# First projection of a decoder trunk: stationary operand from a transposed read of x, the norm's scale put on v, q and k afterwards

## The chip, the cores and the metric

One core of one Trainium2 chip runs the whole program in one launch. The metric is the device time of one execution in microseconds. TensorE is called PE here, its weight loads PEld, VectorE DVE, ScalarE ACT, GpSimd POOL, and the queue that issues most DMAs is SyncE's (SP).

## The reference

The model has two layers over 512 tokens of width 1024. Only the head of layer 0 matters here: an RMSNorm with gain `g[0]`, one projection to q, k, v and 16 forget-gate logits, and attention with 16 heads of width 64.

```
def rmsnorm(x, g):
    y = xf * lax.rsqrt(jnp.mean(xf * xf, axis=-1, keepdims=True) + RMS_EPS)
    return (y * g)

hn = rmsnorm(x, g[0])
proj = hn @ w_in                     # q | k | v | forget logits
q = q * HEAD_DIM ** -0.5
log_f = log_sigmoid(proj[..., 3 * D:] + b_f);  c = cumsum(log_f)
s = q k^T + c_q - c_k, causal;  o = softmax(s) @ v;  return o @ w_out
```

After it come the output projection, an MLP, a gated embedding, and the second layer with a short convolution in the place of attention. All of that is untouched by the change.

## The kernel before, in words

Everything is float32, and every product is taken as three products of halves: a value is split into a rounded high part (`hi`, made by ACT) and a rest (`lo`, made by DVE as source minus `hi`), and `mm3` (L212) issues hi·hi, lo·hi and hi·lo into one accumulator. A weight tile goes the same way: SP fetches a `raw` tile (`fetch`, L113, 14 buffers), and `prepare` (L133) splits it into `wh` and `wl`. `wide` (L150) prepares a tile and up to `soon` tiles ahead of it. SBUF pages of 128x512 come from one pool of 70, PSUM accumulators from 8 banks.

The projection needs the activations with the model width on the partitions. So before the change, for each of the four blocks of 128 tokens, ACT sums the squares of a row-major x tile (`squares`, L243), POOL makes the reciprocal root (`rstd`, L234), DVE multiplies x by it and by the gain (`scaled`, L251), PE turns eight 128x128 squares (`turned`, L259), and ACT and DVE split the result into `hT` (`keep`, L265), a pair of tiles of 128 x 8 x 512. The gain `g0` is spread over the partitions by two PE matmuls of a row of ones with a row of g (L856 to L858), for which POOL's queue loads two rows.

v is made in three column chunks (`V_CHUNKS`, L32): columns 768 to 1023 with the 16 logits (272 wide), 0 to 511 (512 wide), 512 to 767 (256 wide). In each, the token block is stationary and the weight moves: 8 k-tiles x 4 token blocks x 3 products, 96 matmuls. The first chunk is ordered by hand (`manual_schedule`, L568) for PE, DVE and ACT: block t runs its first five k-tiles, then block t+1 is turned, then block t ends. All that follows is ordered by a scheduler that simulates the engines and may move an instruction that is ready ahead of earlier ones in the program.

`keep_v` (L400) adds the bias to the logits and splits v out of PSUM in pieces of 128 columns. `logs` and `sums_of_logs` make the cumulated gates; `bias` loads them, spread over the partitions, for each head. `project(i)` (L418) makes k and then q of a head pair, 24 matmuls of 512 columns each, ACT and DVE splitting each out of PSUM; pairs 1 to 7 are streamed in between the scores, transposes and mixes of the heads.

DMAs at the start are ordered by hand (L850): the first x block by ACT's and SP's queues, then weight tiles and the other x blocks on SP.

Of the kernel before, what the change touches and what calls it, by code (L numbers as in the profile page):

```python
# [8 lines left out]
F32 = mybir.dt.float32  # L9
F32R = mybir.dt.float32r  # L10
AF = mybir.ActivationFunctionType
ALU = mybir.AluOpType
# [3 lines left out]
P = 128  # L16
D = 1024
S = 512
H = 16
HD = 64  # L20
# [18 lines left out]
SCORED = 12  # L39
LEFT = 10  # L40
LATE = 0

# [16 lines left out]


@with_exitstack
def trunk(ctx: ExitStack, tc, x, pT, g, wv, wqk, bf, wo, wci, cw, wco, wup, wdn, wpp, wpg, out):
    nc = tc.nc
    pool = lambda name, bufs, **k: ctx.enter_context(tc.tile_pool(name=name, bufs=bufs, **k))
    consts = pool("consts", 1)
# [10 lines left out]
    def bank(name):  # L78
        return psum.tile([P, S], F32, tag="ps", name=name)
# [70 lines left out]
    def wide(*key, soon=SOON):  # L150

        prepare(where[key] + 1 + soon)
        return ready[key]
# [58 lines left out]
    def mm3(ps, a, b, start, stop):  # L212

        nc.tensor.matmul(ps, a.hi, b.hi, start=start, stop=False)  # L214
        nc.tensor.matmul(ps, a.lo, b.hi, start=False, stop=False)  # L215
        nc.tensor.matmul(ps, a.hi, b.lo, start=False, stop=stop)  # L216
        streamed[0] += 3 * ps.shape[-1]
        due()

    def split(hi, lo, src, eng=nc.vector):  # L220

        nc.scalar.copy(hi, src)  # L222
        eng.tensor_tensor(out=lo, in0=src, in1=hi.bitcast(F32), op=ALU.subtract)  # L223

    def gain(l, i):
        ts = [page(f"g{l}_{i}_{n}") for n in range(2)]
        for n in range(2):
            nc.sync.dma_start(
                ts[n][:, :S],
                g[6 * l + i : 6 * l + i + 1, n * S : (n + 1) * S].partition_broadcast(P),  # L230
            )
        return ts
# [15 lines left out]
    def stats(t, xs, name):  # L248
        return rstd([squares(xs[n][:, :S], f"{name}_q{n}_{t}") for n in range(2)], f"{name}_r{t}")

    def scaled(t, n, xs, r, gB, name):  # L251
        h = page(f"{name}_h{t}_{n}")
        nc.vector.scalar_tensor_tensor(
            out=h[:, :S], in0=xs[n][:, :S], scalar=r, in1=gB[n][:, :S],
            op0=ALU.mult, op1=ALU.mult,
        )
        return h

    def turned(t, n, h, name):  # L259
        ps = bank(f"{name}_p{t}_{n}")  # L260
        for j in range(4):
            nc.tensor.transpose(ps[:, j * P : (j + 1) * P], h[:, j * P : (j + 1) * P], ident)
        return ps

    def keep(t, n, ps, hT):  # L265
        to = lambda h: h[:, 4 * n : 4 * n + 4, t * P : (t + 1) * P]
        split(to(hT.hi), to(hT.lo), ps.rearrange("p (j c) -> p j c", j=4))
# [33 lines left out]
    def load_x(name, t):  # L301
        xs = [page(f"{name}{t}_{n}") for n in range(2)]
        for n in range(2):
            eng = nc.scalar if name == "xa" and n else nc.sync
            eng.dma_start(xs[n][:, :S], x[t * P : (t + 1) * P, n * S : (n + 1) * S])
        return xs

    def tokens_of(pair, t):
# [2 lines left out]
    def tokens(pair, k, t):  # L311
        return pair.at(lambda h: h[:, k, t * P : (t + 1) * P])
# [20 lines left out]
                         f"{kind}r")  # L333
                then(t)

    def attention(hT, first_x, g0, by_hand):
        b_f = consts.tile([P, H], F32, tag="bf", name="b_f")

        vs = [[page(f"v{t}_{i}", F32R) for i in range(4)] for t in range(NB)]
# [43 lines left out]
                )  # L383
                nc.sync.dma_start(neg_c[b, :, :n], t[:H, :n])

        def values(c, t, soon=SOON, between=None):

            c0, width = V_CHUNKS[c]
            n_v = min(width, D - c0)
            ps = bank(f"v{c}_{t}")  # L390
            for k in range(KT):
                if width == 256:
                    w = wide("v", c, k // 2).at(lambda u: u[:, k % 2 * 256 : k % 2 * 256 + 256])
                else:
                    w = wide("v", c, k, soon=soon)
                if k == 5 and between:
                    between()
                mm3(ps[:, :width], tokens(hT, k, t), w, k == 0, k == KT - 1)

            def keep_v():  # L400
                if n_v < width:
                    nc.vector.tensor_tensor(
                        out=logit[:, t * H : (t + 1) * H], in0=ps[:, n_v:width], in1=b_f,
                        op=ALU.add,
                    )
                for c1 in range(0, n_v, 256):
                    src = ps[:, c1 : c1 + 256].rearrange("p (i e d) -> p i e d", e=2, d=HD)
                    block = vs[t][(c0 + c1) // 256].rearrange("p (i r) -> p i r", i=2)
                    for e in range(2):
                        hi = block[:, :, 192 * e : 192 * e + HD]  # L410
                        lo = block[:, :, 64 + 64 * e : 128 + 64 * e]
                        split(hi, lo, src[:, :, e, :])

            return keep_v

        stacked, probs, outs, both = {}, {}, {}, {}

        def project(i):  # L418

            q, key = (Pair(page(f"{n}h{i}", F32R), page(f"{n}l{i}", F32R)) for n in "qk")  # L420
            stacked[i] = q, key
            for s in (1, 0):
                ps = bank(f"qk{i}_{s}")
                for k in range(KT):
                    mm3(
                        ps, narrow("qk", i, k=k, c=s * P),
                        hT.at(lambda h: h[:, k, :]), k == 0, k == KT - 1,
                    )
                    if k < KT - 1:
                        yield  # L430
                if s == 0:
                    nc.scalar.mul(q.hi[:, :S], ps, HD**-0.5)
                    nc.vector.scalar_tensor_tensor(
                        out=q.lo[:, :S], in0=ps, scalar=HD**-0.5, in1=q.hi[:, :S].bitcast(F32),
                        op0=ALU.mult, op1=ALU.subtract,
                    )
                else:
                    split(key.hi[:, :S], key.lo[:, :S], ps)
                yield
# [114 lines left out]
            yield from out_part((0, 1), (6,))  # L554

        nc.sync.dma_start(b_f, bf[0:1, :].partition_broadcast(P))
        name = "n0"
        E, done_v = mybir.EngineType, []

        def rows(t):  # L560
            r = stats(t, first_x[t], name)
            return [scaled(t, n, first_x[t], r, g0, name) for n in range(2)]

        def turn_rows(t, hs):
            for n in range(2):
                keep(t, n, turned(t, n, hs[n], name), hT)

        with tc.manual_schedule(engines={E.PE, E.DVE, E.Activation}):  # L568
            r = stats(0, first_x[0], name)
            prepare(3)  # L570
            hs = {0: [scaled(0, n, first_x[0], r, g0, name) for n in range(2)]}
            prepare(4)
            for n in range(2):
                keep(0, n, turned(0, n, hs[0][n], name), hT)
                prepare(5 + n)
            prepare(KT)
            hs[1] = rows(1)
            hs[2] = rows(2)
            for t in range(NB):
                between = (lambda: turn_rows(t + 1, hs[t + 1])) if t + 1 < NB else None  # L580
                done_v.append(values(0, t, 0, between))
                if t + 3 < NB:
                    hs[t + 3] = rows(t + 3)
                if t:
                    prepare(KT + 3 * t)
                    done_v.pop(0)()
        done_v.pop(0)()
        tri = page("tri", F32R)
        ones = page("ones")
        nc.gpsimd.memset(ones[:, :S], 1.0)  # L590
# [4 lines left out]
        nc.vector.tensor_copy(tri[:, :S], ones[:, :S])  # L595
        logs()
        for t in range(NB):
            values(1, t)()
            if t == 2:
                sums_of_logs(tri)  # L600
        bias(0)
        bias(1)
        for t in range(NB):
            values(2, t)()
        for _ in project(0):
            pass
        main = stream()
# [234 lines left out]
                then(t)  # L842


    one = page("one")
    nc.vector.memset(one[:1, :P], 1.0)
    rows = [page(f"row{n}") for n in range(2)]
    for n in range(2):
        nc.gpsimd.dma_start(rows[n][:1, :], g[0:1, n * S : (n + 1) * S])
    with tc.manual_schedule(engines={mybir.EngineType.SP, mybir.EngineType.Activation}):  # L850
        first_x = [load_x("xa", 0)]
        fetch(4)
        first_x.append(load_x("xc", 1))
        fetch(KT)
        first_x += [load_x("xc", t) for t in (2, 3)]
    g0 = [bank(f"g0_{n}") for n in range(2)]  # L856
    for n in range(2):
        nc.tensor.matmul(g0[n], one[:1, :P], rows[n][:1, :], start=True, stop=True)  # L858
    kept = dram.tile([2, NB, 2, P, S], F32, tag="kept", name="kept")
    hT = turned_x  # L860
    by_hand = ExitStack()
    lhs, opened = attention(hT, first_x, g0, by_hand)
    oT = lhs
    lhs = lambda k, t: tokens(oT, k, t)
    kind = "o"
# [45 lines left out]
def layout(x, p, norm_g, w_attn_in, b_forget, w_attn_out, w_conv_in, conv_w, w_conv_out,  # L911
# [17 lines left out]
    ).reshape(D, 2 * D)  # L929
    got["wqk"] = tiles(qk, 2, 256)  # L930
    got["bf"] = np.asarray(b_forget)
    got["wo"] = tiles(np.asarray(w_attn_out)[0], 1, S)
    b, c, u = (np.asarray(w_conv_in)[0].reshape(D, 3, KT // 2, 2, P)[:, s] for s in range(3))
    ci = np.stack([c[:, :, 0], u[:, :, 0], b[:, :, 0], b[:, :, 1], c[:, :, 1], u[:, :, 1]], axis=2)
# [27 lines left out]
```

## Time and profile before

| what | value |
|---|---|
| median of three runs | 1263.35 us (1263.23 to 1263.46) |
| span of the profiled execution | 1262.1 us |
| what lies around the span (median less span) | 1.25 us |
| PE busy | 1238.7 us, 98% of the span |
| DVE, ACT, POOL busy | 906.1, 604.0, 627.5 us |
| mean granted TensorE clock | 0.997 |
| HBM read, written | 136.93 MB, 6.37 MB |

The profile is one execution. Its span runs from the first instruction to the last. A timeline row gives the start, the length, the engine, the line and the tiles; `x8` means that eight instructions are merged. A matmul's length holds its way through the array and overlaps the next one's, so what one costs in a row of many is the distance between starts.

### The profile page before, as it was taken

The page shows a single profiled execution, that of the slowest core. Times are in us where ns is not written, and L with a number is a line of the kernel's source. Part 1 is how long each engine was busy: PE and PEld are TensorE (multiplying, and loading weights), DVE is VectorE, ACT ScalarE, POOL GpSimd, SP SyncE. Part 2 cuts the span into 40 slices and gives each one's busy share as a digit, 9 for nine tenths or more (in the row PEclk, how much of TensorE's full clock was granted, in tenths as well). Part 3 has the DMA queues.
Part 4 walks back from the last instruction along what each step waited for, and adds up shares of the span by engine and source line. Part 5 has one row for each costly group of instructions (what it writes and reads, how often), then busy time and mean ns, then how long its engine had stood idle before and what let it go on. Part 6 is the DMA issues. An engine that isn't in the chain of part 4 may idle for free.

```text
span 1262.1 us, 18000 instructions
## 1 busy us (share of the span) xinstructions
PE 1238.7 (98%) x6036; PEld 1022.3 (81%) x6036; DVE 906.1 (72%) x1386; ACT 604.0 (48%) x1293; POOL 627.5 (50%) x631
## 2 busy tenths in 40 slices
PE   7999999999999999999999999999999999999997
PEld 6877777788888888888789988889788888888876
DVE  5645666767788788879867444457778897779973
ACT  5445656654645434554455333344653445535451
POOL 2027555328787777876211000016777777878210
PEclk9999999999999999999999999999999999999999
DMA  7554342161432244227333233432323442235401
GB/s 249 152 142 149 100 126 76 62 224 65 134 95 86 87 134 134 84 68 258 126 100 94 74 101 101 141 124 86 94 74 101 134 130 84 71 117 175 159 18 50
DMA packets 83228, 144.48 MB, mean 114 GB/s; under 512 B 9600, under 2 KB 16816, under 8 KB 83136
## 3 DMA queue, kind: packets, MB, share of 16 engines
q1 hardware_dynamic: 82928, 143.07, 36.3%
q8 instruction: 47, 0.77, 0.2%
q14 instruction: 45, 0.37, 0.1%
q10 hardware_dynamic: 144, 0.26, 0.1%
q0 software_dynamic: 64, 0.00, 0.0%
HBM read 136.93 MB, written 6.37 MB: 114 GB/s over the span
## 4 chain that ended last, share of the span: by engine, by line
PE 60%; DVE 18%; POOL 7%; issue 6%; ACT 6%; DMA 3%; SPq 1%; DVEq 0%; POOLq 0%; ACTq 0%
DVE wl L223 10%; POOL s L720 4%; PE up L215 3%; PE up L216 3%; PE up L214 3%; ACT wh L222 3%; PE dn L215 3%; PE qk L214 3%; PE dn L216 3%; PE dn L214 3%; DVE acc L752 2%; PE qk L216 2%; PE qk L215 2%; PE sc L468 2%; PE pg L214 2%
## 5 line engine op out<-in xcount | busy, mean ns | idle before, releaser
L223 DVE TENSOR_TENSOR wl<-raw,wh 128x512 fp32r<-128x512 f32 (+1 forms) x404 | 365.2, 955 | 25.3 <-ACT wh L222 24.6
L222 ACT CAST wh<-raw 128x512 fp32r<-128x512 f32 (+1 forms) x404 | 219.5, 619 | 8.9 <-DVE xd L296 5.0
L215 PE MATMUL up<-hTh,wl 128*128 128x512 f32 (+1 forms) x576 | 210.5, 366 | 0.0
L216 PE MATMUL up<-hTl,wh 128*128 128x512 f32 (+1 forms) x576 | 210.0, 366 | 0.0
L214 PE MATMUL up<-hTh,wh 128*128 128x512 f32 (+1 forms) x576 | 209.7, 366 | 0.0
L223 POOL TENSOR_TENSOR wl<-T,wh 128x512 fp32r<-128x512 f32 x112 | 160.9, 1468 | 35.8 <-ACT wh L222 32.0
L215 PEld LDWEIGHTS up<-hTh,wl 128*128 128x128 f32 x576 | 108.7, 189 | 17.6
L214 PEld LDWEIGHTS up<-hTh,wh 128*128 128x128 f32 x576 | 108.6, 189 | 17.5
L216 PEld LDWEIGHTS up<-hTl,wh 128*128 128x128 f32 x576 | 108.3, 189 | 17.3
L752 DVE TENSOR_TENSOR acc<-dn,acc 128x512 f32<-128x512 f32 x168 | 107.4, 679 | 10.5 <-PE dn L216 10.5
L131 POOL TENSOR_TENSOR T<-raw,raw 128x512 f32<-128x512 f32 x56 | 87.5, 1573 | 37.0 <-DMA raw<-in_wdn 24.8
L706 ACT ACTIVATE r<-up 128x512 f32<-128x512 f32 (+1 forms) x72 | 38.7, 547 | 126.3 <-PE up L216 126.3
L131 POOL TENSOR_TENSOR T<-raw,T 128x512 f32<-128x512 f32 x56 | 91.3, 1631 | 2.2
L692 DVE TENSOR_TENSOR q<-r 128x512 f32<-128x512 f32 (+1 forms) x72 | 66.9, 936 | 29.2 <-ACT r L706 29.2
L237 POOL TENSOR_SCALAR cor_r_v<-cos,cos 128x1 f32<-128x1 f32 x4 | 1.6, 398 | 159.1 <-ACT junk L245 159.1
L222 ACT CAST wh<-T 128x512 fp32r<-128x512 f32 x112 | 61.2, 617 | 0.0
L222 ACT CAST A11h<-q 128x256 fp32r<-128x256 f32 x28 | 11.4, 407 | 99.9 <-DVE q L692 99.9
L214 PE MATMUL pg<-wh,hTh 128*128 128x512 f32 x128 | 50.9, 398 | 3.4 <-ACT hTh L222 3.3
L214 PE MATMUL qk<-hTh,wh 128*128 128x512 f32 x128 | 53.0, 414 | 0.0
L759 POOL TENSOR_TENSOR acc<-acc,acc 128x512 f32<-128x512 f32 x28 | 47.0, 1708 | 10.0 <-DVE acc L752 10.0
L216 PE MATMUL qk<-hTl,wh 128*128 128x512 f32 x128 | 50.8, 397 | 0.0
L215 PE MATMUL qk<-hTh,wl 128*128 128x512 f32 x128 | 50.5, 395 | 0.0
(236 smaller groups left out, 3067.1 us busy)
## 6 DMA issues: line engine op xcount, KB each, us to landing
raw<-in_wup SPq DMA_DIRECT2D x128, 256.0 KB, 2.9
raw<-in_wdn SPq DMA_DIRECT2D x128, 256.0 KB, 2.8
raw<-in_wci SPq DMA_DIRECT2D x48, 256.0 KB, 3.5
raw<-in_wqk SPq DMA_DIRECT2D x32, 256.0 KB, 3.8
raw<-in_wpg SPq DMA_DIRECT2D x32, 256.0 KB, 3.8
g<-in_g SPq DMA_DIRECT2D x22, 256.0 KB, 5.4
prl<-neg_c SPq DMA_DIRECT2D x16, 256.0 KB, 6.7
raw<-in_wo SPq DMA_DIRECT2D x16, 256.0 KB, 2.7
```

The lines of the kernel that those rows point to most:

```text
L131: nc.gpsimd.tensor_tensor(out=B[name, p], in0=B[a, p], in1=B[b, p], op=ALU.subtract)
L214: nc.tensor.matmul(ps, a.hi, b.hi, start=start, stop=False)
L215: nc.tensor.matmul(ps, a.lo, b.hi, start=False, stop=False)
L216: nc.tensor.matmul(ps, a.hi, b.lo, start=False, stop=stop)
L222: nc.scalar.copy(hi, src)
L223: eng.tensor_tensor(out=lo, in0=src, in1=hi.bitcast(F32), op=ALU.subtract)
L468: nc.tensor.matmul(ps[:, :nm], at[r, b * P : n], to[r, :nm], start=s == 0, stop=s == 2)
L692: nc.vector.tensor_tensor(out=out, in0=r, in1=r, op=ALU.mult)
L706: nc.scalar.activation(r[:, :n], ps[:, :n], AF.Relu)
L720: sums = lambda out, a, b, op: nc.gpsimd.tensor_tensor(out=out, in0=a, in1=b, op=op)
L752: nc.vector.tensor_tensor(out=a, in0=banks[s], in1=a, op=ALU.add)
L759: nc.gpsimd.tensor_tensor(out=a, in0=a, in1=acc[i, s][:, :S], op=ALU.add)
```

## The change

The host also hands in x transposed (`xT`, eight tiles of 128 x 512, one for each k-tile, 256 KB each) and the first gain as a column table `g0T`. `hT` for k-tile k is now `xT[k]` times the gain of each partition: ACT multiplies and rounds to `hi`, DVE makes `lo` from the same source (`split_by`). The scale per token is left out of it. The first two v chunks keep four accumulators open, one for each token block, and go k-tile by k-tile (`chunk`): 12 matmuls for each. Row-major x is still loaded, behind the first eight weight tiles, and its sums of squares and `r0[t]` are made during the second chunk. `keep_v` multiplies by `r0[t]`. The four `r0` columns are also written to a DRAM row and read back spread over the partitions as `r_row`, and `project` multiplies q's and k's accumulator by it on DVE into an SBUF page, from which ACT and DVE then split. The row of ones, the gain rows and their matmuls, the 32 transposes of the first norm and their splits are gone. PE gets 16 matmuls of a zeroed page at the very start. The sums of logs move from behind the third block of chunk 2 to behind the second block of chunk 3, and chunk 3 is made block by block behind all of the second chunk's `keep_v`.

```diff
+WARM = 16
+    def split_by(hi, lo, src, by):
+        nc.scalar.mul(hi, src, by)
+        nc.vector.scalar_tensor_tensor(
+            out=lo, in0=src, scalar=by, in1=hi.bitcast(F32), op0=ALU.mult, op1=ALU.subtract
+        )
...
+        def keep_v(c, t, ps):
...
+                nc.vector.scalar_tensor_tensor(
+                    out=logit[:, t * H : (t + 1) * H], in0=ps[:, n_v:width], scalar=r0[t],
+                    in1=b_f, op0=ALU.mult, op1=ALU.add,
+                )
...
+                    split_by(hi, lo, src[:, :, e, :], r0[t])
...
+                scaled_ps = page(f"qk{i}_{s}")[:, :S]
+                nc.vector.tensor_tensor(out=scaled_ps, in0=ps, in1=r_row[:, :S], op=ALU.mult)
+                ps = scaled_ps
...
+        def chunk(c, after):
+            width = V_CHUNKS[c][1]
+            banks = [bank(f"v{c}_{t}") for t in range(NB)]
+            for k in range(KT):
+                if c == 0:
+                    split_by(hT.hi[:, k, :], hT.lo[:, k, :], first_xT[k][:, :S], g0_col[:, k : k + 1])
+                w = wide("v", c, k, soon=0)
+                for t in range(NB):
+                    mm3(banks[t][:, :width], tokens(hT, k, t), w, k == 0, k == KT - 1)
+                after(k)
+            return banks
...
         with tc.manual_schedule(engines={E.PE, E.DVE, E.Activation}):
-            r = stats(0, first_x[0], name)
...
+            banks = {0: chunk(0, lambda k: None)}
+            def between(k):
+                t = k - 1
+                if 0 <= t < NB:
+                    r0[t] = stats(t, first_x[t], "n0")
+                    nc.sync.dma_start(
+                        r_dram[0:1, t * P : (t + 1) * P].rearrange("o s -> s o"), r0[t]
+                    )
+                    if t == NB - 1:
+                        nc.sync.dma_start(r_row[:, :S], r_dram[0:1, :].partition_broadcast(P))
+                if k >= NB:
+                    keep_v(0, k - NB, banks[0][k - NB])
+            banks[1] = chunk(1, between)
...
         for t in range(NB):
-            values(1, t)()
-            if t == 2:
+            keep_v(1, t, banks[1][t])
+        for t in range(NB):
+            values(2, t)
+            if t == 1:
                 sums_of_logs(tri)
         bias(0)
         bias(1)
-        for t in range(NB):
-            values(2, t)()
...
+    warm = page("warm")
+    nc.vector.memset(warm[:, :S], 0.0)
...
+        nc.scalar.dma_start(g0_col, g0T)
+        for k in range(KT):
+            (nc.scalar if k < 2 else nc.sync).dma_start(first_xT[k][:, :S], xT[k])
+            fetch(k + 1)
+        first_x = []
+        for t in range(NB):
+            fetch(KT + t + 1)
+            first_x.append(load_x("xc", t))
+    idle = bank("idle")
+    for _ in range(WARM):
+        nc.tensor.matmul(idle[:, :P], warm[:, :P], warm[:, :P], start=True, stop=True)
```

## Rows read from the trace of the kernel before

**Rows 1.** Waits of PE: engine, line, what for, total us, times, longest.

```profile
PE g L858 <- DMA row<-in_g: 6.0, 1, 6.0
```

**Rows 2.** Windows: length, busy us of each engine, granted clock, DMA share, GB/s.

```profile
11.43:65.59 54.16, 52.14 (x322) 47.19 (x321) 35.08 (x87) 28.95 (x77) 6.58 (x16) 0.97 0.60 193
65.59:300.00 234.41, 232.59 (x1244) 182.16 (x1243) 153.60 (x384) 132.94 (x331) 113.51 (x177) 1.00 0.39 123
300.00:1240.00 940.00, 934.26 (x4403) 778.91 (x4402) 707.35 (x899) 434.13 (x868) 502.72 (x424) 1.00 0.35 108
1240.00:1262.10 22.10, 14.23 (x63) 11.46 (x61) 6.98 (x10) 3.37 (x8) 1.72 (x4) 0.93 0.12 47
```

**Rows 3.** Timeline of PE over the projection of v: start us, length us, then names.

```profile
5.96 3.75 PE L858 MATMUL g<-row,one 1*128 1x512 f32 x4 [5.96 <-DMA row<-in_g]
...
11.43 0.59 PE L214 MATMUL v<-wh,hTh 128*128 128x272 f32 x1
...
13.00 0.35 PE L215 MATMUL v<-wh,hTl 128*128 128x272 f32 x1
...
16.50 1.96 PE L262 MATMUL n_p<-ident,n_h 128*128 128x128 f32 x8 [1.89 <-DVE n_h L253]
...
18.72 0.43 PE L216 MATMUL v<-wl,hTh 128*128 128x272 f32 x1
...
19.62 0.43 PE L214 MATMUL v<-wh,hTh 128*128 128x272 f32 x1
...
33.06 0.30 PE L216 MATMUL v<-wl,hTh 128*128 128x272 f32 x1
...
35.70 0.29 PE L216 MATMUL v<-wl,hTh 128*128 128x272 f32 x1
...
47.38 0.40 PE L371 MATMUL ps_c<-tri,lf_h 128*16 128x512 f32 x1
...
48.55 0.44 PE L214 MATMUL v<-wh,hTh 128*128 128x512 f32 x1
48.84 0.39 PE L215 MATMUL v<-wh,hTl 128*128 128x512 f32 x1
...
54.08 0.28 PE L214 MATMUL v<-wh,hTh 128*128 128x256 f32 x1
...
65.59 0.40 PE L214 MATMUL qk<-hTh,wh 128*128 128x512 f32 x1
```

**Rows 4.** DMA from 0 to 30 us: rate in 40 slices of 0.75 us; one issue.

```profile
GB/s 0 0 19 48 143 380 383 383 400 370 371 317 328 351 238 249 287 361 355 402 404 407 404 393 391 377 348 379 382 268 74 0 0 22 22 224 153 265 341 52
...
xa<-in_x SPq DMA_DIRECT2D x1, 256.0 KB, 4.4
```

**Rows 5.** ACT and DVE prices near the new operations: min/median/max ns, or busy us, mean ns.

```profile
L664 ACT ACTIVATE za<-z,taps x10: 508/724/725, 690.6 to 807.4; 128x512 f32<-128x512 f32 x6, 128x256 f32<-128x256 f32 x4
...
L253 DVE SCALAR_TENSOR_TENSOR n_h<-xc,n_r_y,g 128x512 f32<-128x512 f32 x6 | 4.2, 745 | 3.4 <-POOL n_r_y L240 3.3
...
L223 DVE TENSOR_TENSOR wl<-raw,wh 128x272 fp32r<-128x272 f32 x8 | 3.2, 436 | 6.4 <-ACT wh L222 6.4
```

**Rows 6.** Timelines of SP and ACT: a DMA of line 637, weight casts, a piece of v.

```profile
16.09 0.33 SPq L637 DMA_DIRECT2D taps<-in_cw  x1
...
38.73 2.69 ACT L222 CAST wh<-raw 128x512 fp32r<-128x512 f32 x5
...
46.52 0.27 ACT L222 CAST v<-v 128x128 fp32r<-128x128 f32 x1 [0.36 <-DVE v L223]
```

**Rows 7.** Timelines of DVE and PE: q of pair 1 ready, its first score.

```profile
91.52 0.69 DVE L433 SCALAR_TENSOR_TENSOR ql<-qk,qh 128x512 fp32r<-128x512 f32 x1 [0.32 <-ACT qh L432]
...
94.28 0.39 PE L468 MATMUL sc<-kh,qh 64*128 64x256 f32 x2
```

**Rows 8.** Groups by line and shape from 78 to 260 us, DVE and POOL: busy us, mean ns.

```profile
L223 DVE TENSOR_TENSOR wl<-raw,wh 128x512 fp32r<-128x512 f32 x43 | 28.8, 702 | 5.5 <-ACT wh L222 5.1 <-issue 0.4
...
L480 POOL TENSOR_SCALAR prl<-prl,rs 128x512 f32<-128x512 f32 x16 | 25.5, 1593 | 13.4 <-DVE rs L479 13.0
```

More of the change, by code (lines that the diff above doesn't have):

```diff
@@ L63, in trunk @@
 @with_exitstack
-def trunk(ctx: ExitStack, tc, x, pT, g, wv, wqk, bf, wo, wci, cw, wco, wup, wdn, wpp, wpg, out):
+def trunk(ctx: ExitStack, tc, x, xT, pT, g, g0T, wv, wqk, bf, wo, wci, cw, wco, wup, wdn, wpp, wpg, out):
     nc = tc.nc
@@ L303, in load_x @@
         for n in range(2):
-            eng = nc.scalar if name == "xa" and n else nc.sync
-            eng.dma_start(xs[n][:, :S], x[t * P : (t + 1) * P, n * S : (n + 1) * S])
+            nc.sync.dma_start(xs[n][:, :S], x[t * P : (t + 1) * P, n * S : (n + 1) * S])
         return xs
@@ L334, in mixer_out, with attention @@
                 then(t)
-    def attention(hT, first_x, g0, by_hand):
+    def attention(hT, first_xT, g0_col, first_x, by_hand):
         b_f = consts.tile([P, H], F32, tag="bf", name="b_f")
@@ L384, in sums_of_logs, with values @@
                 nc.sync.dma_start(neg_c[b, :, :n], t[:H, :n])
-        def values(c, t, soon=SOON, between=None):
+        def keep_v(c, t, ps):
             c0, width = V_CHUNKS[c]
             n_v = min(width, D - c0)
+            if n_v < width:
+                nc.vector.scalar_tensor_tensor(
+                    out=logit[:, t * H : (t + 1) * H], in0=ps[:, n_v:width], scalar=r0[t],
+                    in1=b_f, op0=ALU.mult, op1=ALU.add,
+                )
+            for c1 in range(0, n_v, 256):
+                src = ps[:, c1 : c1 + 256].rearrange("p (i e d) -> p i e d", e=2, d=HD)
+                block = vs[t][(c0 + c1) // 256].rearrange("p (i r) -> p i r", i=2)
+                for e in range(2):
+                    hi = block[:, :, 192 * e : 192 * e + HD]
+                    lo = block[:, :, 64 + 64 * e : 128 + 64 * e]
+                    split_by(hi, lo, src[:, :, e, :], r0[t])
+        def values(c, t):
             ps = bank(f"v{c}_{t}")
             for k in range(KT):
[L392 to L414, printed above, removed]
+                w = wide("v", c, k // 2).at(lambda u: u[:, k % 2 * 256 : k % 2 * 256 + 256])
+                mm3(ps[:, :256], tokens(hT, k, t), w, k == 0, k == KT - 1)
+            keep_v(c, t, ps)
         stacked, probs, outs, both = {}, {}, {}, {}
@@ L556, in attention @@
         nc.sync.dma_start(b_f, bf[0:1, :].partition_broadcast(P))
[L557 to L566, printed above, removed]
-        with tc.manual_schedule(engines={E.PE, E.DVE, E.Activation}):
-            r = stats(0, first_x[0], name)
[L570 to L578, printed above, removed]
-            for t in range(NB):
[L580 to L586, printed above, removed]
@@ L587, in attention @@
-        done_v.pop(0)()
+        E = mybir.EngineType
+        r0 = {}
+        r_dram = dram.tile([1, S], F32, tag="r_dram", name="r_dram")
+        r_row = page("r_row")
+        def chunk(c, after):
[9 more added lines that the diff above has]
+            return banks
@@ L602, in attention @@
         bias(1)
-        for t in range(NB):
-            values(2, t)()
         for _ in project(0):
@@ L842, in ple @@
                 then(t)
[L845 to L849, printed above, removed]
-    with tc.manual_schedule(engines={mybir.EngineType.SP, mybir.EngineType.Activation}):
[L851 to L858, printed above, removed]
+    g0_col = consts.tile([P, KT], F32, tag="g0_col", name="g0_col")
+    warm = page("warm")
+    nc.vector.memset(warm[:, :S], 0.0)
+    first_xT = [page(f"xT{k}") for k in range(KT)]
+    with tc.manual_schedule(engines={mybir.EngineType.SP, mybir.EngineType.Activation}):
+        nc.scalar.dma_start(g0_col, g0T)
[9 more added lines that the diff above has]
+        nc.tensor.matmul(idle[:, :P], warm[:, :P], warm[:, :P], start=True, stop=True)
     kept = dram.tile([2, NB, 2, P, S], F32, tag="kept", name="kept")
@@ L861, in trunk @@
     by_hand = ExitStack()
-    lhs, opened = attention(hT, first_x, g0, by_hand)
+    lhs, opened = attention(hT, first_xT, g0_col, first_x, by_hand)
     oT = lhs
@@ L931, in layout @@
     got["bf"] = np.asarray(b_forget)
+    got["xT"] = got["x"].reshape(S, KT, P).transpose(1, 2, 0)
+    got["g0T"] = np.asarray(norm_g)[0, 0].reshape(KT, P).T
     got["wo"] = tiles(np.asarray(w_attn_out)[0], 1, S)
```

## The prediction

> **What bounds the kernel now.** I read the waits of PE first, then windows over the whole span, then PE's timeline at the start. PE waits for almost nothing in the trace but its start: 6.0 us for the gain rows is its longest wait [rows 1]. In the windows it is busy for 232.59 of 234.41 us from the first q/k product to 300 us and for 934.26 of 940.00 us up to 1240 us [rows 2]. So from 65.59 us on, where the projection of q and k begins [rows 3], PE sets the time, and whatever moves that first q/k product moves the end by about as much. What follows it up to the end is 1196.5 us that the change hardly touches (only q, k and their page).
>
> The stage to cost is therefore from 0 to 65.59 us. PE's timeline [rows 3] shows three things there. The first v product starts at 11.43 us, behind x, its norm, the gain matmuls and the first transposes. PE waits again before 16.50 us, for the second block's scaled rows, and then turns it. And the clock is low in two spells: products of 272 columns start 0.225 us apart from 18.72 to 19.62 us (four gaps), at the level of 1.2 GHz, and 0.126 us apart from 33.06 to 35.70 us (21 gaps), at 2.4 GHz.
>
> **What stays of that stage.** 96 products in each chunk. 272 columns: 96 x 0.1257 = 12.1 us. 512 columns: 23 gaps from 48.84 to 54.08 us, 0.2278 each, 21.9 us. 256 columns: from 54.08 to 65.59 us, all 96, 11.5 us. The sums of logs: 47.38 to 48.55 us, 1.2 us [rows 3]. Together 46.7 us of PE at the full clock, the same before and after. Before, the stage from 11.43 us takes 54.16 us [rows 2]; the 7.5 us on top are the transposes of three blocks, the wait before 16.50 us and the low clock.
>
> **When the products can start now.** Two things must be there.
>
> The operands: xT[0] is the second DMA that ACT issues, so it goes out about when SP's x tile did before, which landed 4.4 us after its issue and let ACT start at about 5.6 us. ACT's multiply with a scale per partition out of SBUF costs 0.72 us (the row of line 664), DVE's `lo` 0.745 us (line 253, two tensors and a scalar), and the weight's split at most 0.44 us on each engine [rows 5]. The chain to the third product is 5.6 + 0.72 + 0.745 + 0.44 = 7.5 us; two products lie before it, so the stream behaves as if it began at 7.25 us.
>
> The warm-up: PE takes its 16 matmuls first, in order. Before, two float32 matmuls of 512 columns show as four records in 3.75 us [rows 3], so one instruction is two passes, about 0.87 us per 512 columns or 0.22 per 128 at the low level. 32 passes are 7 us at that level. They begin when DVE has filled the page, at about 1.4 us. The clock rose at 13.00 us after PE had been at work from 5.96 us, and by 19.85 us after work from 16.50 us [rows 3]: 7.0 us and 3.4 us. If it rises 3.4 us in, the warm-up ends at 1.4 + 3.4 + 1.8 = 6.6 us; if 7 us in, at 8.4 us. I take a start of the full-clock stream at 7.6 us, between 7.25 and 8.4.
>
> **Does anything hold the stream up afterwards?** A k-tile of the first chunk is 12 x 0.1257 = 1.51 us of PE. It needs ACT for 0.72 + 0.44 and DVE for 0.745 + 0.44 us, both under 1.2, and 256 + 136 KB, which at about 380 GB/s take 1.06 us [rows 4, 5]. From a first byte at 3.3 us the eighth k-tile is in by 11.8 us and is wanted at 7.6 + 7 x 1.51 = 18.2 us. A k-tile of the second chunk is 12 x 0.2278 = 2.7 us of PE for one weight tile; with row-major x between the tiles, all of it (6.35 MB) is in by about 20 us, and PE gets to the second chunk at 19.7 us. 9 banks are asked of 8, but the ninth replaces the warm-up's, idle by then.
>
> Row-major x, its squares and `r0` come behind the weights, off PE's path. SP's queue gets four writes of r0, each of which waits for POOL, and one read back that waits for all four; weight fetches queued behind them would wait too. The scheduler moves a ready DMA forward: one of line 637, the convolution's, goes out at 16.09 us [rows 6]. So I cost this at nothing. r_row is in by some 20 + 2.5 (squares and root) + 2 x 4.4 = 31 us and is first read at the end of the first k projection, near 60 us; with that cover gone it would cost what it is late. The multiplication by r0 changes a copy into a multiply and a subtract into a fused one, of the same shape.
>
> The 16 new multiplies by r_row are 16 x 0.69 = 11 us of DVE, which is busy for 153.6 of 234.4 us in that window [rows 2]. On the path they are a later q: `ql` of pair 1 ends at 91.52 + 0.69 = 92.2 us and its first score starts at 94.28 [rows 7], 2.07 us of slack, against 0.69 for the multiply and 0.1 for ACT. Cost zero, at most a few tenths for each of the seven pairs.
>
> **A rule that speaks against it.** After the change `kl` and `ql` read two SBUF operands where one was in PSUM. Weight splits, which read two, take 702 ns in this stretch, beside POOL at work in between with 1593 ns for its longest scaling [rows 8]; so the row puts the loss at about 0.01 us each, and were each to wait for one whole scaling, q would be 0.69 + 0.1 + 1.6 = 2.4 us later, 0.3 us past pair 1's slack.
> The Trainium skill ("SBUF — State Buffer", Who interferes with whom) says that a DVE instruction with two SBUF inputs and a GpSimd instruction that reads SBUF share a read port, and the later one waits in full. By that rule the sum would be 0.3 us worse; by the row it is not.
>
> **The sum.** First q/k product at 7.6 + 46.7 = 54.3 us in the place of 65.59: 11.3 us less. The span becomes 1250.8 us, and with the 1.25 us that lie between span and median, 1252.0 us.
>
> **Rivals.**
> 1. *The warm-up does not hold the clock.* It streams zeros, and the low spells above began after idle time. If the clock is low when the products start, at 8.4 us, each us of low clock loses 0.44 us (1 - 0.1257/0.225). A spell of 1.6 us (11.43 to 13.00) to 7.0 us loses 0.7 to 3.1: first q/k product at 55.8 to 58.2, 1253.6 to 1256.0 us. For it: 7.0 us of work before the first rise. Against: both spells ended with PE at work.
> 2. *The third chunk's weights come late.* `chunk` prepares no tile ahead (`soon=0`), and in program order the tiles of the third chunk stand behind all 16 pieces of the second chunk's `keep_v`. A piece costs ACT 0.27 + 0.36 us, as its next waits for DVE [rows 6], so in that order PE stands still for up to 16 x 0.63 = 10.1 us and loses clock: 1262 to 1263 us, no gain. Half of it: 1257. Against: ACT takes five weight casts at 38.73 us, ahead of pieces of v such as the one at 46.52 [rows 6].
> 3. *Slower: q and k come late.* DVE runs in order, and the multiply by r_row stands in front of `kl`, `ql` and of the score reductions. It would eat the 11.3 us if each of seven pairs made PE wait 1.6 us, for pair 1 a q later by 3.7 us, not 0.8. With a wait of 2 us each the time is 1252.0 + 14 = 1266 us. Against: DVE has a third of its time free.
> 4. *More than forecast.* PE also loses 234.41 - 232.59 = 1.8 us in the attention [rows 2], and the order there is made anew. With that gone and a start at 7.25 us: 1249.8 us.
>
> **How the numbers follow.** Forecast 0.62 (1250 to 1253.5), rival 1 0.17, rival 2 0.09 (half of it under 1260), rival 3 0.05, rival 4 0.07. The likeliest is 1252.0 us. The range reaches down to rival 4's 1249.8 with a little for a fresh order, 1249, and up past rival 1's bound to 1257, where half a rival 2 lies; what is left out is the rest of rivals 2 and 3. Faster by over 0.2% (2.5 us, about what a measurement of this kernel can tell from no change): 0.91; within it 0.04; slower 0.05.
>
> **What would show it.** Right: the first v product near 7 us with products 0.126 us apart from there, no wait of PE up to the first q/k product near 54 us, and that product as much earlier as the end is. Rival 1: 0.225 us apart at the start. Rival 2: a hole in PE between chunks two and three. Rival 3: scores that wait for DVE's `ql`. The prediction fails most plainly if PE's start moves and its later idle time grows by as much.

## The result, and the profile after

The changed kernel takes 1265.28 us (median of 20 runs, 1264.53 to 1266.32), the kernel before, timed beside it, 1263.36 us: a ratio of 1.0016, 95% interval [1.001, 1.0022]. That is 0.16% slower and not the 11.3 us faster that were forecast. The profiled execution's span is 1263.3 us against 1262.1.

PE's waits in the changed kernel, which answer to [rows 1], name the largest part of the loss. The wait for the gain rows is gone, and one as long stands elsewhere:

```profile
PE v L215 <- ACT wh L223: 6.7, 2, 6.0
```

PE's timeline says where. It is the view of [rows 3]:

```profile
1.50 5.26 PE L868 MATMUL idle<-warm 128*128 128x128 f32 x32 [1.50 <-DVE warm L855]
7.51 0.39 PE L215 MATMUL v<-wh,hTh 128*128 128x272 f32 x1 [0.74 <-ACT wh L223]
...
8.57 0.29 PE L215 MATMUL v<-wh,hTh 128*128 128x272 f32 x1
8.70 0.28 PE L216 MATMUL v<-wh,hTl 128*128 128x272 f32 x1
...
41.78 0.39 PE L217 MATMUL v<-wl,hTh 128*128 128x512 f32 x1
48.16 0.58 PE L215 MATMUL v<-wh,hTh 128*128 128x256 f32 x1 [5.99 <-ACT wh L223]
48.54 0.42 PE L216 MATMUL v<-wh,hTl 128*128 128x256 f32 x1
48.76 0.41 PE L215 MATMUL v<-wh,hTh 128*128 128x256 f32 x1
...
52.28 0.32 PE L217 MATMUL v<-wl,hTh 128*128 128x256 f32 x1
...
62.86 0.40 PE L215 MATMUL qk<-hTh,wh 128*128 128x512 f32 x1
```

The start is the forecast one: the first product at 7.51 us, products 0.125 us apart from 8.57 us, two chunks without a gap. Then no product runs from 42.17 (41.78 + 0.39) to 48.16 us, and what follows is 0.22 us apart, where products of this shape stand 0.12 us apart at 2.4 GHz: the clock is at 1.2 GHz until 52.28 us. So the first q/k product comes at 62.86 us in the place of 65.59, 2.7 us earlier and not 11.3.

The windows of [rows 2] in the changed kernel, and two short ones around the hole (the granted clock is the number behind the five engines):

```profile
7.51:62.86 55.35, 49.27 (x296) 43.66 (x297) 34.93 (x85) 34.97 (x84) 5.10 (x10) 0.94 0.76 234
62.86:300.00 237.14, 235.36 (x1233) 184.12 (x1232) 162.62 (x399) 133.45 (x328) 120.01 (x184) 1.00 0.39 124
...
45.00:50.00 5.00, 1.83 (x6) 1.24 (x7) 3.80 (x11) 4.01 (x11) 0.00 (x0) 0.55 0.68 207
50.00:55.00 5.00, 5.00 (x34) 4.46 (x33) 5.00 (x9) 4.10 (x8) 0.00 (x0) 0.77 0.89 254
```

ACT's timeline in the hole shows what PE waits for. The third chunk's first weight cast stands behind 15 of the 16 pieces of the second chunk's v, and eight of these wait for DVE's rest of the one before:

```profile
40.17 0.37 ACT L228 ACTIVATE v<-v,n_r_y 128x128 fp32r<-128x128 f32 x1 [4.17 <-PE v L217]
...
47.24 0.37 ACT L228 ACTIVATE v<-v,n_r_y 128x128 fp32r<-128x128 f32 x1 [0.42 <-DVE v L229]
47.51 0.61 ACT L223 CAST wh<-raw 128x512 fp32r<-128x512 f32 x1
48.03 0.37 ACT L228 ACTIVATE v<-v,n_r_y 128x128 fp32r<-128x128 f32 x1
48.29 5.81 ACT L223 CAST wh<-raw 128x512 fp32r<-128x512 f32 x11
```

The raw tiles are not what is late. SP asks for the third chunk's four long before, and tiles of this size landed 4.6 us after their issue in the median:

```profile
21.50 1.98 SPq L120 DMA_DIRECT2D raw<-in_wv  x4
```

A second loss comes later, in a stretch where PE waits for nothing. From the first score to the first output product the kernel before takes 130.1 us, the changed one 134.9. From the first `up` product to the end both take 983.6 us (1262.1 - 278.46 and 1263.3 - 279.70).

The table gives, for every kernel of this study, the starts of the first v, q/k, score and output product in its profile, the stretch between the last two, and the timed runs. Each difference and each ratio is against runs of the kernel before on the same chip.

| kernel | v | q/k | score | out | score to out | median us | minus before | ratio, 95% |
|---|---|---|---|---|---|---|---|---|
| before | 11.43 | 65.59 | 82.03 | 212.14 | 130.1 | 1263.36 | | |
| after | 7.51 | 62.86 | 79.30 | 214.15 | 134.9 | 1265.28 | +1.9 | 1.0016 [1.001, 1.0022] |
| 1 weights early | 7.58 | 54.81 | 71.25 | 207.40 | 136.2 | 1258.12 | -5.5 | 0.9957 [0.9942, 0.9971] |
| 2 before + multiply | 11.42 | 64.68 | 81.12 | 215.95 | 134.8 | 1268.12 | +4.5 | 1.0036 [1.0023, 1.0049] |
| 3 after, no multiply | 8.09 | 63.45 | 79.89 | 209.92 | 130.0 | 1262.22 | -1.4 | 0.9988 [0.9978, 0.9997] |
| 4 after, order by hand | 7.84 | 64.03 | 80.47 | 204.65 | 124.2 | 1254.67 | -8.9 | 0.9927 [0.9912, 0.9942] |
| 5 weights early, no multiply | 7.60 | 54.31 | 70.75 | 200.78 | 130.0 | 1252.99 | -10.5 | 0.9919 [0.9903, 0.9936] |
| 6 weights early, by hand | 7.91 | 54.60 | 71.04 | 199.97 | 128.9 | 1248.17 | -15.6 | 0.9875 [0.9859, 0.9892] |
| 7 before, by hand | 11.43 | 64.66 | 81.10 | 203.83 | 122.7 | 1255.21 | -8.6 | 0.9932 [0.9917, 0.9947] |
| 8 as 6, no warm-up | 7.60 | 56.94 | 73.38 | 198.19 | 124.8 | 1249.65 | -14.2 | 0.9889 [0.9874, 0.9904] |
| 9 as 2, by hand | 11.93 | 65.17 | 81.61 | 207.06 | 125.5 | 1257.75 | -6.1 | 0.9953 [0.9938, 0.9967] |
| 10 as 6, gates early | 7.73 | 54.96 | 71.40 | 196.31 | 124.9 | 1247.00 | -16.5 | 0.9869 [0.9854, 0.9884] |
| 11 as 10, no multiply | 7.40 | 54.61 | 71.05 | 193.70 | 122.7 | 1244.48 | -19.0 | 0.9849 [0.9834, 0.9864] |
| 12 as 10, zeroing on DVE | 7.87 | 55.13 | 71.57 | 194.44 | 122.9 | 1245.51 | -18.3 | 0.9855 [0.9838, 0.9871] |

### The profile page after: what moved, and what is told of

Its sections match the earlier page's. It is cut to its first block, busy times and chain, and to the rows that moved or that the text cites. A ratio compares the mean times of both kernels' runs of the same rounds, so it can differ in the third digit from the quotient of the medians.

```text
span 1263.3 us, 17998 instructions
## 1 busy us (share of the span) xinstructions
PE 1239.7 (98%) x6032; PEld 1024.0 (81%) x6032; DVE 913.1 (72%) x1394; ACT 609.2 (48%) x1293; POOL 631.7 (50%) x629
## 4 chain that ended last, share of the span: by engine, by line
PE 84%; DVE 7%; ACT 3%; issue 2%; POOL 2%; DMA 1%; SPq 0%; DVEq 0%; POOLq 0%; ACTq 0%
PE up L216 8%; PE up L217 8%; PE up L215 8%; PE dn L216 6%; PE dn L217 6%; PE dn L215 6%; PE qk L215 3%; PE sc L473 3%; DVE wl L224 3%; PE qk L217 2%; PE qk L216 2%; PE pg L215 2%; PE pg L217 2%; PE pg L216 2%; PE pT L492 1%
## 5 line engine op out<-in xcount | busy, mean ns | idle before, releaser
L700 DVE TENSOR_TENSOR q<-r 128x512 f32<-128x512 f32 (+1 forms) x72 | 69.7, 975 | 28.5 <-ACT r L714 28.3
```

The lines of the kernel that those rows point to most:

```text
L700: nc.vector.tensor_tensor(out=out, in0=r, in1=r, op=ALU.mult)
```

## The experiments

**1. The third chunk's weights early.** Its tiles are split inside the hand-ordered block, ahead of the second chunk's `keep_v`.

```diff
             banks[1] = chunk(1, between)
+            prepare(where["v", 2, KT // 2 - 1] + 1)
```

> The changed kernel with the four weight tiles of the third v chunk split right behind the second chunk, ahead of that chunk's keep_v pieces. Theory A (ACT and DVE take 15 pieces of keep_v before the first weight of chunk 3, PE stands idle for 6.0 us and then runs at the low clock): the first q/k product moves from 62.86 to about 54.5 us and the time falls by about 8 us, to 1257. Rival B (ACT and DVE are simply full there, and PE would wait for a PSUM bank or for the next weights instead): the hole moves, the time falls by 3 us at most, to 1262.

The hole is gone and the clock stays up: the first q/k product comes at 54.81 us, 8.05 us earlier than in the changed kernel. Of these, 6.0 are the wait, and some 1.8 the low clock behind it (4.1 us of PE's work, 48.16 to 52.28, with products 0.22 apart in the place of 0.12). The time falls by 7.4 us, from +1.9 to -5.5 against before. The hole is shown to be the first loss. The second stays: 136.2 us from score to output, 1.3 more than in the changed kernel, of which 1.04 is a new wait of PE at 91.48 us (see experiment 6).

**2. The multiply alone, in the kernel before.** Only the DVE multiply of each q and k accumulator is added, by a row of ones.

```diff
+        one_row = page("one_row")
+        nc.gpsimd.memset(one_row[:, :S], 1.0)
...
+                scaled_ps = page(f"qk{i}_{s}")[:, :S]
+                nc.vector.tensor_tensor(out=scaled_ps, in0=ps, in1=one_row[:, :S], op=ALU.mult)
+                ps = scaled_ps
```

> The kernel before with one addition: q's and k's accumulators are multiplied on DVE by a row of ones and split from that SBUF page, 16 more DVE instructions and nothing else of the change. Theory A (the extra step alone lengthens the attention, through the order that the scheduler gives PE): first score to first output product grows from 130.1 to about 134.9 us, the time to about 1268. The prediction's step (hidden in 2 us of slack): 1263.4, no change. Rival B (the attention is longer because it starts earlier, with its gates and masks not there yet): no change either.

It costs 4.5 us, and the stretch from score to output takes 134.8 us, as in the changed kernel. So the multiply is the second loss, without anything else of the change.

**3. The changed kernel without it.** This leaves out the norm's scale on q and k.

```diff
-                scaled_ps = page(f"qk{i}_{s}")[:, :S]
-                nc.vector.tensor_tensor(out=scaled_ps, in0=ps, in1=r_row[:, :S], op=ALU.mult)
-                ps = scaled_ps
```

> The changed kernel without the multiplication of q and k by r_row: the norm's scale per token is left out of q and k. Theory A: the attention goes back to about 130 us from first score to first output product, the hole ahead of chunk 3 stays, time 1260.5. Rival B: the attention stays at 134.9 us, time 1265.

The stretch is back at 130.0 us. The time falls by 3.3 us, less than the 4.8 expected: its first v product came 0.58 us later, its hole is as long, and from the first output to the first `up` product it took 66.35 us, the changed kernel 65.55.

What is PE's part in it? The scores of a pair's two heads are each 64 rows high and lie side by side in the array. PE's timeline of the changed kernel:

```profile
157.40 0.38 PE L473 MATMUL sc<-kh,qh 64*128 64x256 f32 x1
157.62 0.28 PE L473 MATMUL sc<-kl,qh 64*128 64x256 f32 x1
157.74 0.27 PE L473 MATMUL sc<-kh,ql 64*128 64x256 f32 x1
157.95 0.50 PE L515 MATMUL ps_o<-pl,v 128*128 128x512 f32 x1
158.38 0.38 PE L473 MATMUL sc<-kh,qh 64*128 64x256 f32 x1
...
158.92 0.50 PE L215 MATMUL qk<-hTh,wh 128*128 128x512 f32 x1
```

And the same place of a pair in the kernel before, where the two heads' products share a row (`x2`):

```profile
137.62 0.39 PE L468 MATMUL sc<-kh,qh 64*128 64x256 f32 x2
137.84 0.28 PE L468 MATMUL sc<-kl,qh 64*128 64x256 f32 x2
137.96 0.28 PE L468 MATMUL sc<-kh,ql 64*128 64x256 f32 x2
138.17 0.50 PE L214 MATMUL qk<-hTh,wh 128*128 128x512 f32 x1
```

Six products side by side take 0.55 us (137.62 to 138.17); three of one head alone take as long (157.40 to 157.95, and again 158.38 to 158.92). A mix that slips in between the heads makes PE do the same work twice as slowly, without a wait in any view. Summed over the stretch by the distance to the next start, the score products take 25.3 us before and 28.7 after; in the place of 39 spots where another kind follows a score there are 45. Experiment 2 has 28.7 us and 45 spots, experiment 3 has 25.3 and 39. So 3.4 of the 4.7 us are the order of the scores; by the same sum, transposes take 1.1 us more and mixes 0.5.

**4. PE's order by hand.** All 78 steps of the attention's loop, in the place of the last four, are given to PE in the order of the program, which keeps the two heads together.

```diff
-BY_HAND = 2
+BY_HAND = 4 * 16 + 12
```

> The changed kernel with PE's order in the whole attention written out by hand (BY_HAND = 76 in the place of 2), so that the score products of a head pair stand side by side; all operations are the same, the r_row step is kept. If the loss in the attention is PE's order alone: about 4 us less, 1261, with no new wait of PE. If it is the load on DVE: PE now waits in order for DVE, time 1265 or more.

More than expected: 124.2 us, 5.9 less than in the kernel before. The score products take 18.8 us, at 27 spots of change. The DVE work is all there, so a full DVE is not what held the changed kernel. Its hole stayed, at 6.0 us.

**5. Both failed steps taken back, and nothing else** (edits 1 and 3; the norm's scale on q and k is left out again).

> The changed kernel with the third chunk's weights split early and without the multiply by the scale row, PE's order left to the scheduler (left out: the first norm's scale on q and k). Both steps in which the prediction failed are taken back, and nothing else is changed, so the prediction's remaining sum is tried as it was put: the first q/k product at 54.8 us (predicted 54.3), the stretch from there to the end as before, 1252.0 us (1251 to 1253.6). If a third loss is hidden behind the two, such as gates that come late, the first score to the first output product takes 132 us or more and the time is 1254 us or more.

The rest of the forecast holds: first q/k product at 54.31 us, forecast 54.3, and 1252.99 us, forecast 1252.0. No third loss is hidden here: the stretch takes 130.0 us, as before the change.

**6. Both repairs with all operations** (edits 1 and 4).

> The changed kernel with both repairs and no operation left out: the third chunk's weight tiles are split inside the hand-ordered block, and PE's order over the attention is written by hand. Theory (a): the two losses are separate, the hole of 6 us with its spell of low clock ahead of the first q/k product, and the order of the score products. Then the gains add: the first q/k product comes at 54.8 us as in the kernel with early weights, the stretch from the first score to the first output product takes 124 to 125 us as in the one with the hand-written order, and the time is 1246 us (1245 to 1248). Theory (b): the hole hid something that the attention waits for, such as the gates or the scale row; then PE waits show in the first scores and the time stays at 1249 us or more.

1248.17 us, just above the range of theory (a), and the runs spread more than others (1247.44 to 1251.2; the profile is of the longest). Theory (b) is right in part. Its PE and POOL timelines:

```profile
91.65 0.33 PE L492 MATMUL pT<-ident,prl 128*128 128x128 f32 x1 [1.76 <-POOL prl L485]
...
93.11 0.63 PE L216 MATMUL qk<-hTh,wl 128*128 128x512 f32 x1
93.54 0.63 PE L217 MATMUL qk<-hTl,wh 128*128 128x512 f32 x1
```

```profile
86.07 0.77 POOL L459 TENSOR_SCALAR_AFFINE_SELECT prr<-prr 128x128 f32<-128x128 f32 x1 [1.69 <-DMA prr<-neg_c]
...
90.03 3.10 POOL L485 TENSOR_SCALAR prl<-prl,rs 128x512 f32<-128x512 f32 x2
```

PE waits for a scaling in POOL's queue and then runs q/k products 0.43 us apart, the 1.2 GHz level, up to 96.26 us. With q and k 8 us earlier, the gates are what comes late next: POOL waits 1.69 us for a gate page to land from DRAM, masks it, and only then goes on to the scalings that stand behind it in its queue.

**7. The kernel before with the hand order** (edit 4).

> The kernel before the change, with PE's order over the attention written by hand. Theory (a), the order is a gain of its own that the change has no part in: the stretch from the first score to the first output product takes 124 to 125 us in the place of 130.1, first q/k product still at 65.6 us, and the time is 1257.5 us (1257 to 1259). The difference to the kernel with both repairs is then what the change is worth with PE's order held equal: the 11.3 us of the prediction, or 10.8 by the first q/k product at 54.8. Theory (b), the hand order only repairs what the change spoiled: no gain here, 1263 us.

1255.21 us, better than expected: the order is worth 8.6 us by itself, and the change has no part in it. It is the yardstick for what follows. Between experiments 7 and 6 lie 7.0 us, for a first q/k product that is 10.1 us earlier.

**8. As 6, without the warm-up.**

```diff
-WARM = 16
+WARM = 0
```

> The kernel with both repairs, without the 16 warm-up products. The operands are there at about 7.5 us with or without them. If the warm-up is what gives the full clock at the first v product, products are 0.225 us apart for a spell of 3.4 to 7 us of PE work, each us losing 0.44: the first q/k product is 1.5 to 3.1 us later and the time 1248 to 1249 us. If the clock is at its upper level without it, the time is within 0.5 us of the kernel with both repairs.

Its PE timeline:

```profile
7.60 0.59 PE L215 MATMUL v<-wh,hTh 128*128 128x272 f32 x1 [7.60 <-ACT wh L223]
...
9.05 0.43 PE L216 MATMUL v<-wh,hTl 128*128 128x272 f32 x1
9.28 0.43 PE L217 MATMUL v<-wl,hTh 128*128 128x272 f32 x1
...
13.28 0.28 PE L217 MATMUL v<-wl,hTh 128*128 128x272 f32 x1
13.40 0.29 PE L215 MATMUL v<-wh,hTh 128*128 128x272 f32 x1
```

0.227 us apart up to 13.1 us, 0.125 from 13.28. The first q/k product is 2.3 us later than in experiment 6, within what was expected, so the warm-up does hold the clock. The time, 1249.65 us, is 0.7 above the expected range, and only 1.5 above experiment 6, with overlapping intervals: PE does not wait for `prl` here, so experiment 6 gives part of its earlier start back to the gates.

**9. The multiply in the kernel before, with the hand order** (edits 2 and 4).

> The kernel before the change with the added DVE multiply of q's and k's accumulator (by a row of ones) and PE's order over the attention written by hand. If the multiply costs only through the order that is made anew, the time is that of the kernel before with the hand order, 1257.5 us, within 1 us, and the two stretches from first score to first output product agree within 1 us. If the multiply makes PE wait by itself, it is slower by 3 to 5 us as it was without the hand order, with PE waiting for DVE's ql or for the split probabilities.

Between the two theories: 2.5 us over experiment 7 (1257.75 against 1255.21), where it was 4.5 without the hand order. So something over half of the multiply's price stays when PE's order is held, and the rest goes with PE's order that was made anew. With that order held the score products take 18.9 us with the multiply and 18.8 without, so the 2.5 us sit elsewhere (experiment 12).

**10. The gates early.** The sums of logs go ahead of the third chunk.

```diff
         for t in range(NB):
+            if t == 0:
+                sums_of_logs(tri)
             values(2, t)
-            if t == 1:
-                sums_of_logs(tri)
```

> The kernel with both repairs, and the sums of logs ahead of the third chunk's first block in the place of behind its second, so that the gates are written and read back earlier. In the kernel with both repairs the first gates are read from DRAM at 59.7 us, five microseconds after their writes were issued, and POOL, which masks them and scales the first probabilities, is in work or waits for them from 82 to 105 us; PE waits 1.8 us for POOL's prl at 91 us and loses clock. Theory (a), the wait is the gates' lateness, which the hole of the changed kernel covered: the gates are read some 5 us earlier, PE no longer waits for prl, the stretch from the first score to the first output product goes from 128.9 us to 125 us, and the time is 1245.5 us (1244.5 to 1247). Theory (b), POOL is simply full at the start of the attention: the wait stays, and the time is 1247.5 to 1248.5 us.

The first gate is read at 53.73 us in the place of 59.68, PE's wait for `prl` is gone, the stretch takes 124.9 us and the time is 1247.00, at the upper end of theory (a)'s range. The medians differ by 1.2 us with overlapping intervals, so the trace, not the time, carries this reading.

**11. As 10, without the multiply** (edit 3; the scale on q and k is left out).

> The same, without DVE's multiply of q's and k's accumulator by the scale row (left out: the first norm's scale on q and k). The prediction costed that multiply at nothing; the kernel before with the hand order lost 2.5 us to it. If that price is the same here, the time is 1243 us (1242 to 1244) and the stretch from first score to first output product 122.7 us, as in the kernel before with the hand order and no multiply; the difference to that kernel, 1255.2 us, is then the whole of what the first q/k product comes earlier, 10 us of the 11.3 predicted. If the multiply is hidden here, it is within 0.7 us of the kernel that has it.

1244.48 us: the multiply costs 2.5 us here too, and the stretch is that of experiment 7 (122.7 us). Against experiment 7 the time is 10.4 us less (19.0 - 8.6, each against before) for a first q/k product 10.05 us earlier. That is the forecast's step "moves the end by as much", measured.

**12. Zeroing on DVE.** Where do the 2.5 us sit? In experiment 10's POOL and PE timelines, once in a pair:

```profile
110.91 0.29 POOL L459 TENSOR_SCALAR_AFFINE_SELECT prl<-prl 128x128 f32<-128x128 f32 x1 [0.96 <-DMA prl<-neg_c]
111.19 0.92 POOL L485 TENSOR_SCALAR pr<-pr,rs 128x256 f32<-128x256 f32 x1
112.07 0.29 POOL L459 TENSOR_SCALAR_AFFINE_SELECT pr<-pr 128x128 f32<-128x128 f32 x1
112.30 0.20 POOL L499 MEMSET ph<- 128x128 f32 x1
```

```profile
111.86 0.27 PE L492 MATMUL pT<-ident,prl 128*128 128x128 f32 x1
112.56 0.19 PEld L514 LDWEIGHTS ps_o<-ph,v 128*128 128x128 f32 x1 [0.66 <-POOL ph L499]
112.56 0.39 PE L514 MATMUL ps_o<-ph,v 128*128 128x256 f32 x1 [0.42 <-DVE nmx L479]
```

PE wants the split probabilities whose unused corner POOL zeroes, and the zeroing stands behind a scaling and two masks. The product's wait is put down to DVE's `nmx`, that of its weight load to POOL's zeroing of `ph`. The edit moves the zeroing:

```diff
-                    nc.gpsimd.memset(z[:, lo_q : j * P].bitcast(F32), 0.0)
+                    nc.vector.memset(z[:, lo_q : j * P].bitcast(F32), 0.0)
```

> The kernel with early weights, hand order and early gates, with the zeroing of the unused corner of the split probabilities (two 128x128 pages' worth for each head) moved from POOL to DVE. With PE's order held, the multiply by the scale row cost 2.5 us, and PE's extra idle time stands once in each head pair, 0.3 to 0.7 us before the first mix of a head's fourth block, whose corner POOL zeroes behind a scaling of 0.9 us that waits for DVE. Theory (a): that wait is the price, DVE's lateness reaching PE through POOL's queue; with the zeroing taken off that queue the four waits of 1.7 us in all go, and the time is 1245.4 us (1245 to 1246.2). Theory (b): DVE's own order is what is late, and the zeroing on it changes nothing or adds to it: 1247 us or more.

In five places of experiment 10 a mix starts 0.31 to 0.70 us after the last transpose ahead of it. Four of these are gone here, and no distance but the fifth's (0.56 us; 0.51 in experiment 11) is over 0.28. The stretch takes 122.9 us and the time is 1245.51 us, as theory (a) has it.

Theory (a)'s mechanism is only half right, though: the scaling does not wait for DVE. It needs one of two reciprocals, and both are there by 108.68 us:

```profile
108.53 0.15 DVE L484 RECIPROCAL rs<-sm 128x1 f32<-128x1 f32 x1
```

It stands in POOL's queue behind the mask of `prl`, which waits for its read from DRAM. Without the multiply (experiment 11) the scaling stands ahead of that mask, and the zeroing right behind it:

```profile
109.02 0.92 POOL L482 TENSOR_SCALAR pr<-pr,rs 128x256 f32<-128x256 f32 x1
110.22 0.29 POOL L456 TENSOR_SCALAR_AFFINE_SELECT prl<-prl 128x128 f32<-128x128 f32 x1 [0.28 <-DMA prl<-neg_c]
110.45 0.20 POOL L496 MEMSET ph<- 128x128 f32 x1
```

In the four pairs looked at, the kernels with the multiply (after, experiments 1, 2, 4, 6, 8, 9 and 10) all have the first order and those without it (before, 3, 5, 7 and 11) the second. So the multiply had POOL's order made anew too, and the zeroing came to stand further back.

This kernel leaves no operation out and beats both kernels: 18.3 us less than before, ratio 0.9855 [0.9838, 0.9871].

## Why the prediction was wrong, step by step

- **What stays of the stage: right; its start: right, in part by luck.** 46.7 us of PE from 7.6 us was the forecast; experiment 5 has 54.31 - 7.60 = 46.7. But 7.6 had been taken between two terms, 7.25 and 8.4, and the first was short: ACT began its first multiply at 6.43 us in the changed kernel, not at 5.6, because it loaded a function table for 1.28 us behind its wait for `xT` (before, ACT did that at 1.23 us, while x was on its way). The warm-up ended at 6.76 us in the changed kernel, at the early end of 6.6 to 8.4, so rival 1 is out; experiment 8 shows the low clock that it would have brought. In the other eight kernels with the warm-up its last product starts between 6.80 and 7.88 us, and in six of them PE goes on to the first v product without a wait, so warm-up and operands come close together.
- **"Does anything hold the stream up afterwards?" failed.** This is rival 2, held at 0.09 and priced at up to 10.1 us; it cost 8.05 (experiment 1). What spoke against it was misread. The five casts at 38.73 us [rows 6] were taken for casts moved ahead of v pieces. But in the kernel before `wide` prepares eight tiles (`SOON`) during a block's products, ahead of that block's `keep_v`, so they stood there in the program already. The one row that shows a move is a DMA on SP. The trace has a move of casts as well, but of another kind: the same five went ahead of the split of the logs (41.76 us), whose input came last from DVE. Of the third chunk's casts, one passed one piece in the changed kernel. Why the scheduler left the others is not shown.
- **The multiply, "cost zero, at most a few tenths for each of the seven pairs": failed.** It cost 4.5 us, 0.64 a pair. The slack of 2.07 us for pair 1's q was looked for in the right queue, and PE's waits have no `ql` in any run: rival 3 had the sign and not the mechanism. The price went by the order of two other engines. PE's was made anew with the heads apart, which experiments 2 to 4 show together; rival 4 named that order, but as a gain. POOL's was made anew with the zeroing further back: 2.5 us with PE's order held (experiments 9 and 11), and 0.7 to 1.0 with the zeroing moved as well (18.3 against 19.0 us below the kernel before, or 1245.51 less 1244.48; the moved zeroing without the multiply was not tried). That both orders changed because the scheduler's simulation counts the multiply on DVE is argued, not shown.
- **The scale row: cost nothing, but not as worked out.** Forecast in at 31 us, its read went out at 42.28 us and landed at 47; SP stood still for 12 us with weight fetches behind it. The first multiply ran at 68.5 us, so the cover held.

SP's issues in the changed kernel, and the issue-to-landing times of the writes (KB each, median us):

```profile
29.91 0.33 SPq L587 DMA_DIRECT2D r_dram<-n_r_y  x1
42.28 0.33 SPq L591 DMA_DIRECT2D r_row<-r_dram  x1
42.66 1.37 SPq L120 DMA_DIRECT2D raw<-in_wqk  x3
```

```profile
r_dram<-n_r_y SPq DMA_DIRECT2D x4, 0.5 KB, 9.8
```

- **The sum.** The forecast 1252.0, with 8.05 for the hole and 4.5 for the multiply, gives 1264.6; measured 1265.3. Of the 0.7 us left, some 0.5 is the term of 1.25 us around the span: it set the span of one execution against the median of others, and a run with its own span beside it shows 1.7 (1265.03 and 1263.3).

## What to carry to other kernels

A row that seems to show a scheduler moving work shows it only if that work stands later in the program; read the program's order before pricing a step at nothing by it. When an order is made by a simulated time, an instruction added on an idle-looking engine can cost the busy one through the order alone, its own or that of an engine that it waits for. Look for pairs that run side by side and have come apart, which no table of waits shows, and compare each queue's order before and after. When a stage gets shorter, ask of each input of the next stage when it lands, not only of the one that was moved.

## What the runs showed of the hardware

**POOL waits for DVE's second SBUF operand.** POOL masks a 128x128 page in 0.29 us. In the changed kernel `kl` reads two SBUF pages, and a mask that starts within it lasts until it is over:

```profile
160.43 0.69 DVE L224 TENSOR_TENSOR kl<-qk,kh 128x512 fp32r<-128x512 f32 x1 [0.34 <-ACT kh L223]
```

```profile
160.48 0.80 POOL L459 TENSOR_SCALAR_AFFINE_SELECT pr<-pr 128x128 f32<-128x128 f32 x1 [1.21 <-DMA pr<-neg_c]
```

In the kernel before, at the same place of a pair, `kl` reads PSUM and the mask is not held:

```profile
160.72 0.69 DVE L223 TENSOR_TENSOR kl<-qk,kh 128x512 fp32r<-128x512 f32 x1
```

```profile
160.85 0.29 POOL L454 TENSOR_SCALAR_AFFINE_SELECT pr<-pr 128x128 f32<-128x128 f32 x1 [1.34 <-DMA pr<-neg_c]
```

The prediction weighed this from DVE's side alone, by the mean of the weight splits, and found nothing; `kl` and `ql` do stay at a median of 0.69 us. The wait is inside POOL's instruction. The rule named there, in the Trainium skill ("SBUF — State Buffer", Who interferes with whom), says that the later of the two waits in full; the trace agrees, 0.80 us against 0.29. Beside weight splits, such masks of 0.56 to 0.83 us stand in the kernel before too. Over all 64 masks one takes 0.36 us in the mean against 0.34, 1.2 us in sum, and no run here sets their price in time apart.

**A short wait can cost the clock too.** In experiment 6 PE stood still for 1.76 us in the middle of a stream and its products were then at the 1.2 GHz level for 3.6 us (92.63 to 96.26). After the wait of 1.04 us at the same place in experiment 1 they stayed at the upper level, 0.23 us apart.

**Small writes land late.** The four writes of 128 values of 4 bytes took 8.8 to 12.4 us to land, the read of the scale row behind them, 256 KB over all partitions, 4.8.
